# A hybrid attention block on one core: the written order around the MLA heads revised

## The chip, the core and the metric

The kernel runs on one core of one Trainium2 chip. The metric is the device time of one execution in microseconds; of several runs the median counts. Five engines work beside each other, each on its own queue, in order: TensorE (PE, with its weight loads PEld), VectorE (DVE), ScalarE (ACT), GpSimd (POOL) and SyncE (SP), which issues most of the transfers.

## The reference

One layer over 512 tokens of width 1024. The part that matters here is the attention block:

```python
h = rms_norm(x, attn_norm_g)
z = h @ w_in            # q-latent 256 | kv-latent 128 | rope key 32 | diff q 512 | diff k 512 | diff v 512
q = rms_norm(rms_norm(q_lat) @ w_uq);  k, v = (rms_norm(kv_lat) @ w_ukv) ...   # 8 MLA heads
probs = softmax(where(allowed, q k^T * scale, -1e30));  y_mla = probs @ v
q, k = rms_norm(dq), rms_norm(dk)                                              # 4 differential heads
logits = q k^T * scale + bias[t5_bucket(k_idx - q_idx)]                        # for m in (0, 1)
y_diff = rms_norm((probs[0] - lam * probs[1]) @ dv) * (1 - lam_init)
x = x + concat[y_mla, y_diff] @ w_out
```

A query sees the keys of its own and earlier chunks of 64. Behind it follow the convolutional feed-forward block and the gated embedding, which the change leaves alone. All products are kept to fp32 accuracy by splitting an operand into a rounded part and a remainder (`hi`, `lo`) and multiplying three times.

## The kernel before

Tokens lie in four tiles t of 128. The kernel begins with the latents (`zA`, banks for 416 columns of z), the up-projections of the MLA heads (`ukv`, `uq`) and the norms of their q and k. Then come the MLA heads in four pairs hp = 0 to 3, each with four query tiles t, so 16 steps i = 4 hp + t. One step, in the order in which the loop writes it:

- `mla_norm` scales the probabilities `pm` of tile t by the reciprocal of their sums (DVE). With t = 0 or 1 both heads of a pair lie in one bank and one reciprocal does for both; with t = 2 or 3 there are two of one column each.
- `mla_logits` multiplies the logits `ml` of tile t + 1 (PE), takes the row maxima (DVE), and `mla_exp` takes the exponentials (ACT), with their sums.
- At t = 2 and t = 3 PE transposes q and k of the next pair's two heads (`qT`, `kT`, or for the last pair `d0T`, `d1T` of the first diff head); ACT writes the rounded half into the tile `st`, DVE the remainder.
- Then stands what the table `extra` names for the step, a number of units of filling work for PE (`FILL_MLA`, by `pump`), and what `late` names.
- `mla_T` transposes the probabilities into one of the two banks `tp` (`pTm`), and a copy takes them to `pt`: on DVE for the pair's first head or t = 0, on ACT otherwise. `pt` has two buffers, and so has `tp`, which `qT`, `kT`, `d0T`, `d1T` and `pTm` share. `mla_pv` multiplies the probabilities of the step before with v, into the bank `mo`.

The filling work is z's diff columns (`zd_units`): q is `zd0*`, k `zd1*`, v `zd2*`, one tile for each t. A unit is six matmuls into one bank. When a tile is complete `zd_out` copies it out of the bank on ACT (`zd`), and for q and k squares it (ACT, `sq`) and sums the squares by head (DVE, `ssd`). Sums, a root on POOL (`zd_root`, a power, written to `rd`) and a scaling on DVE (`zd_scale`) make the norm. The weights come in tiles of 512 KB (`raw_d`, three buffers shared with `raw_o`), of which ACT makes the rounded half (`hi_d`) and DVE the remainder (`lo_d`), five buffers of each; W_out's are `raw_o`, `hi_o`, `lo_o` (o00 to o03 for the MLA half, o10 to o13 for the diff half).

`bias_strip` makes the diff heads' bias from a small table: 27 small POOL instructions into `vb` (a buffer of the pool of `sq`, which has two), three transfers on POOL's queue (to DRAM, spread over DRAM, back as `strip`), and a memset. `zd_root`'s power stands behind it on POOL.

Then come the 16 diff tiles (h, t), the logits two tiles ahead (`diff_logits`): DVE adds the bias and takes minima, ACT the exponentials, DVE combines the two maps (`pmd`, by `cf`). Between them the units are those of W_out (`wo_units`, banks `o`), for which `yh` and `yl` hold the two halves of the heads' outputs: 0 to 3 for MLA (`ym`, or the bank `mo3` for the last pair), 4 to 7 for diff.

What sets the order: PE's is the written one everywhere. In the region from the start to the line `region.__exit__` those of DVE, ACT and POOL are the written ones too; behind it a scheduler places them, and it may also put later instructions, such as the casts of W_out, between those of the region.

Of the kernel before, what the change touches and what calls it, by code (L numbers as in the profile page):

```python
# [12 lines left out]
F32R = mybir.dt.float32r  # L13
# [9 lines left out]
NT = 4  # L23
# [71 lines left out]
def hybrid_block(ctx: ExitStack, tc: tile.TileContext, a: dict, out: bass.AP):  # L95
# [294 lines left out]
    ssd, rd = small("ssd", [P, 2, NT, 8]), small("rd", [P, 2, NT, 8])  # L390
    def zd_out(c, t, ps):
        z_ = tt(f"zd{c}{t}")
        S.activation(z_, ps, AF.Identity, scale=rx[:, t:t + 1])
        zd[c].append(z_)
        if c < 2:
            sq = sq_tile("sq")[:, :T]
            S.activation(sq, z_, AF.Square)
            V.reduce_sum(ssd[:, c, t, :], sq.rearrange("p (m d) -> p m d", d=64), axis=AX.X)

    def zd_root(c):  # L400
        rms(up(rd[:, c]), up(ssd[:, c]), 8 * NT, 64)
# [196 lines left out]
    def mla_norm(hp, t):  # L598

        pm, pmf, sums, one = mla["pm", hp, t]  # L600
        ssum, rcp = sums[:, 1], sums[:, 2]
        for c in range(2):
            if not (c and one):
                w = slice(0, 2) if one else slice(c, c + 1)
                V.reciprocal(rcp[:, w], ssum[:, w])
            V.tensor_scalar(pm[c], pm[c], rcp[:, c:c + 1], None, op0=ALU.mult)

    def mla_T(hp, t):
# [100 lines left out]
    def diff_logits(h, t):  # L709
# [6 lines left out]
        for m in range(2):  # L716
            r = slice(64 * m, 64 * m + 64)
            ps = bank("lg", f"dl{h}{t}{m}")
            mm3(ps[:, :n], [(qh_[r, tsl[t]], ql_[r, tsl[t]], kh_[r, :n], kl_[r, :n])])
            pm = pm_tile("pmd")  # L720
            nm = sm.tile([P, 1], F32, tag="nm", bufs=4, name="nmd")
            V.tensor_tensor_reduce(out=pm[:, :n], in0=ps[:, :n], in1=strips[0][:, h, T - n:], scale=1.0, scalar=3e38, op0=ALU.add, op1=ALU.min, accum_out=nm)
            S.activation(pm[:, :n], pm[:, :n], AF.Exp, bias=nm, scale=-1.0, accum_out=s0 if m == 0 else s1)
            pms.append(pm)

        cf = sm.tile([P, 1], F32, tag="cf", bufs=4, name="cf")
        V.reciprocal(cf, s1)
        V.scalar_tensor_tensor(cf, cf, nlam, s0, op0=ALU.mult, op1=ALU.mult)
        V.scalar_tensor_tensor(pms[0][:, :n], pms[1][:, :n], cf, pms[0][:, :n], op0=ALU.mult, op1=ALU.add)
        df["pm", h, t] = pms[0]  # L730

    def diff_pv(h, t):
# [44 lines left out]
    def z2_hi(kq):  # L777
# [29 lines left out]
    mla_q(1)  # L807
    pump()
    mla_k(1)
    pump()  # L810
    mla_logits(0, 0)
    for c in range(2):
        mla_exp(0, 0, c)
    for hp in range(HP):
        for t in range(NT):
            i = NT * hp + t
            last = hp == HP - 1
            n = FILL_MLA[t]
            if t:
                mla_norm(hp, t)  # L820
            if t < NT - 1:
# [31 lines left out]
    pump(100)  # L853
    fill.append(wo_units(0, range(4), 4))
    diff_logits(0, 1)
    diff_T(1, 1)
    mla_pv(HP - 1, NT - 1)
    pump()
    y_hl(3, mla["po"])
    for i, (h, t) in enumerate(dslots):  # L860
        if i + 2 < len(dslots):
            diff_logits(*dslots[i + 2])
        pump(FILL_DIFF[h][t])
        df["pt", h, t] = probs_T(df.pop(("pm", h, t)), (t + 1) * P, f"d{h}{t}", True)
        if i:
# [672 lines left out]
```

## Time and profile before

| | us |
|---|---|
| runs, median of 3 (lowest, highest) | 648.82 (647.75, 649.01) |
| the profiled execution | 647.4 |
| its span, first to last instruction | 645.4 |
| PE busy | 633.0 |
| DVE busy | 486.7 |
| ACT busy | 360.6 |

The profile is one execution. The first two numbers of a row of instructions are its start and its duration, both in us from the span's start; an arrow in brackets says for how long the engine had been idle before it and what ended that. Matmuls overlap each other, so the distance between two starts, not the duration, says what a matmul takes of PE's time. The 16 MLA steps lie between about 71 and 161 us, the diff tiles between about 161 and 225 us.

### The profile page before, as it was taken

To read this page: it belongs to the slowest core of one execution; us is meant where nothing else is said; L and a number is where in the kernel's file an instruction comes from. 1 tells how busy PE (TensorE), PEld (TensorE's weight loads), DVE (VectorE), ACT (ScalarE), POOL (GpSimd) and SP (SyncE) were. 2 spreads that over 40 slices of the span, in tenths; PEclk is the share of its full clock that TensorE was granted. 3 is DMA by queue.
4 is the path that set the end of the run, shared out by engine and by line. 5 is a ranking of instruction groups with operands and counts; after the bars stand their busy time and mean duration, and the time that the engine had idled before them with its cause. 6 is when DMAs were issued, how large, how long until landed. Compare 5 with 4: busy or idle time off the path is not lost.

```text
span 645.4 us, 10213 instructions
## 1 busy us (share of the span) xinstructions
PE 633.0 (98%) x3900; PEld 555.6 (86%) x3900; DVE 486.7 (75%) x878; ACT 360.6 (56%) x629; POOL 67.3 (10%) x94
## 2 busy tenths in 40 slices
PE   9999998999999999999999999999999999999997
PEld 8988776887778887889999999999999999988886
DVE  6889666968878768888876767676767676769844
ACT  7897556548676364647554545555464545537211
POOL 1510044300000121001000000000011000000000
PEclk9999999999999999999999999999999999999999
DMA  8251222332410437636775646564646463531121
GB/s 299 104 164 39 92 76 104 99 131 73 125 34 2 163 107 236 164 72 175 190 202 130 180 118 186 127 191 115 180 115 180 115 180 115 180 130 53 39 89 50
DMA packets 29912, 82.63 MB, mean 128 GB/s; under 512 B 3100, under 2 KB 4124, under 8 KB 29736
## 3 DMA queue, kind: packets, MB, share of 16 engines
q1 hardware_dynamic: 23816, 69.17, 32.1%
q0 software_dynamic: 5616, 12.33, 11.3%
q8 instruction: 31, 0.51, 0.3%
q10 hardware_dynamic: 432, 0.49, 0.2%
q14 instruction: 17, 0.14, 0.1%
HBM read 77.77 MB, written 5.52 MB: 129 GB/s over the span
## 4 chain that ended last, share of the span: by engine, by line
PE 78%; DVE 9%; ACT 5%; DMA 4%; POOL 2%; issue 2%; ACTq 0%; DVEq 0%; POOLq 0%
PE dn L158 6%; PE dn L157 6%; PE dn L159 6%; PE gx L159 4%; PE gx L158 4%; PE gx L157 4%; PE g L157 3%; PE g L158 3%; PE g L159 3%; PE o L157 3%; PE o L159 2%; PE o L158 2%; PE pg L157 2%; PE pg L158 2%; PE pg L159 2%
## 5 line engine op out<-in xcount | busy, mean ns | idle before, releaser
L923 DVE TENSOR_TENSOR wSl<-rS,wSh 128x1024 fp32r<-128x1024 f32 x21 | 25.7, 1224 | 43.5 <-ACT wSh L919 43.3
L157 PE MATMUL dn<-ah,hi_dn 128*128 128x512 f32 x144 | 56.2, 391 | 0.0
L158 PE MATMUL dn<-al,hi_dn 128*128 128x512 f32 x144 | 56.2, 391 | 0.0
L159 PE MATMUL dn<-ah,lo_dn 128*128 128x512 f32 x144 | 56.0, 389 | 0.0
L1040 POOL DMA_DIRECT2D rS<-in_w_gu x19 | 22.7, 1194 | 250.4 <-DVE cv L1208 130.0
L919 ACT CAST wSh<-rS 128x1024 fp32r<-128x1024 f32 x21 | 22.0, 1047 | 35.8 <-PE gy L158 35.5
L157 PE MATMUL zd<-hi_d,xh 128*128 128x512 f32 x96 | 39.3, 410 | 0.0
L158 PE MATMUL zd<-lo_d,xh 128*128 128x512 f32 x96 | 37.7, 392 | 0.2 <-DVE lo_d L305 0.2
L674 DVE TENSOR_TENSOR x<-x,dn 128x512 f32<-128x512 f32 x44 | 29.9, 679 | 6.1 <-PE dn L159 6.1
L923 DVE TENSOR_TENSOR wTl<-rA,wTh 128x1024 fp32r<-128x1024 f32 x19 | 23.3, 1225 | 14.0 <-ACT wTh L919 13.5
L159 PEld LDWEIGHTS dn<-ah,lo_dn 128*128 128x128 f32 x144 | 27.0, 188 | 5.7
L157 PEld LDWEIGHTS dn<-ah,hi_dn 128*128 128x128 f32 x144 | 27.1, 188 | 5.2
L158 PEld LDWEIGHTS dn<-al,hi_dn 128*128 128x128 f32 x144 | 27.1, 188 | 4.9
L923 DVE TENSOR_TENSOR wAl<-rA,wAh 128x1024 fp32r<-128x1024 f32 x21 | 25.6, 1217 | 2.6 <-ACT wAh L919 2.6
L919 ACT CAST wAh<-rA 128x1024 fp32r<-128x1024 f32 x21 | 22.1, 1051 | 9.7 <-DMA rA<-in_w_gu 9.2
L1211 ACT ACTIVATE cv<-cv 128x512 f32<-128x512 f32 x22 | 13.9, 630 | 23.9 <-DVE cv L1208 23.8
L596 ACT ACTIVATE pm<-ml,sums,rq 128x128 f32<-128x128 f32 (+3 forms) x32 | 19.6, 617 | 13.4 <-DVE sums L579 8.6
L157 PE MATMUL g<-b2h,wAh 128*128 128x256 f32 (+1 forms) x88 | 26.4, 300 | 0.5 <-ACT g L1164 0.5
L157 PE MATMUL o<-yh,hi_o 128*128 128x512 f32 x64 | 26.9, 420 | 0.0
L159 PE MATMUL g<-b2h,wAl 128*128 128x256 f32 (+1 forms) x88 | 26.2, 297 | 0.0
L158 PE MATMUL g<-b2l,wAh 128*128 128x256 f32 (+1 forms) x88 | 26.2, 297 | 0.0
L1431 ACT ACTIVATE sg<-sg 128x512 f32<-128x512 f32 (+1 forms) x9 | 5.3, 584 | 36.8 <-DVE sg L1430 36.8
(475 smaller groups left out, 2215.7 us busy)
## 6 DMA issues: line engine op xcount, KB each, us to landing
rA<-in_w_gu SPq DMA_DIRECT2D x22, 512.0 KB, 4.0
rS<-in_w_gu SPq DMA_DIRECT2D x22, 512.0 KB, 3.7
rS<-in_w_gu POOLq DMA_DIRECT2D x19, 512.0 KB, 6.0
raw_dn<-in_w_down SPq DMA_DIRECT2D x18, 512.0 KB, 6.0
raw_d<-in_w_d SPq DMA_DIRECT2D x12, 512.0 KB, 4.1
r<-in_w_gu SPq DMA_DIRECT2D x19, 256.0 KB, 6.0
raw_o<-in_w_out SPq DMA_DIRECT2D x8, 512.0 KB, 3.7
rS_pg<-in_w_pg SPq DMA_DIRECT2D x6, 512.0 KB, 4.1
```

The costliest lines, as they stand in the source:

```text
L157: TE.matmul(ps, xh, wh, start=first and i == 0, stop=False, skip_group_check=again)
L158: TE.matmul(ps, xh, wl, start=False, stop=False, skip_group_check=again)
L159: TE.matmul(ps, xl, wh, start=False, stop=last and i == n - 1, skip_group_check=again)
L596: S.activation(pm[c], ps[c], AF.Exp, bias=nm[:, c:c + 1], scale=r[:, c:c + 1], accum_out=sums[:, 1, c:c + 1])
L674: V.tensor_tensor(xb(b), xb(b), ps, op=ALU.add)
L919: S.copy(h_, src)
L923: V.tensor_tensor(l_, src, _f32(h_), op=ALU.subtract)
L1040: nc.gpsimd.dma_start(sums[f].rearrange("p (i c) -> p i c", i=2), a["w_gu"][f][:, :2048].rearrange("p (i c) -> p i c", i=2)[:, :, :512], a ...
L1211: S.activation(cv, cv, AF.Silu)
L1431: S.activation(sg, sg, AF.Sigmoid)
```

## The change

Filling units: the number per step is now a table by pair and tile, two in every step of the first three pairs and one in every step of the last. Before it was 2, 1, 2, 2 in each pair. The number of units is the same; three go from the last pair to the three before.

Copies of z: those of k and v stand behind the copy of the transposed probabilities of the same step. The squares and sums of q and k move to steps 3 to 10, their scalings to steps 8 to 13 (before: squares with the copy, scalings in steps 6 to 12). The cast of z's last k weights goes ahead of the first exponentials.

GpSimd: the strip is made in step 0 (before: step 3).

Reciprocals: one for both heads in every step, behind the second head's sums.

First diff tiles: the written order of DVE, ACT and POOL reaches past the first two diff tiles, whose combination becomes a function of its own, and past the splits of the MLA outputs, which are written one by one. W_out's first weights are cast in steps 8 and 9; the remainder of a further one stands on DVE behind a tile's combination.

```diff
-FILL_MLA = (2, 1, 2, 2)
+FILL_MLA = ((2, 2, 2, 2), (2, 2, 2, 2), (2, 2, 2, 2), (1, 1, 1, 1))
     def zd_out(c, t, ps):
         z_ = tt(f"zd{c}{t}")
-        S.activation(z_, ps, AF.Identity, scale=rx[:, t:t + 1])
         zd[c].append(z_)
-        if c < 2:
-            sq = sq_tile("sq")[:, :T]
-            S.activation(sq, z_, AF.Square)
-            V.reduce_sum(ssd[:, c, t, :], sq.rearrange("p (m d) -> p m d", d=64), axis=AX.X)
+        zouts.append(lambda: S.activation(z_, ps, AF.Identity, scale=rx[:, t:t + 1]))
+        if c == 0:
+            z_flush()
...
+    def zd_sq(c, t):
+        sq = sq_tile("sq")[:, :T]
+        S.activation(sq, zd[c][t], AF.Square)
+        V.reduce_sum(ssd[:, c, t, :], sq.rearrange("p (m d) -> p m d", d=64), axis=AX.X)
...
         for c in range(2):
-            if not (c and one):
-                w = slice(0, 2) if one else slice(c, c + 1)
-                V.reciprocal(rcp[:, w], ssum[:, w])
+            if c == 0:
+                V.reciprocal(rcp, ssum)
             V.tensor_scalar(pm[c], pm[c], rcp[:, c:c + 1], None, op0=ALU.mult)
...
             w = wo_w(kq, dq)
+            if kq == 0 and dq + 1 in dqs:
+                with tc.issue_after(df["comb"].ins):
+                    wo_first[0, dq + 1] = wo_w(0, dq + 1)
...
     extra = {
-        0: [lambda: lo(*z1_hi(3))],
-        3: [bias_strip],
-        4: [lambda: zd_root(0), lambda: z2_hi(0)],
-        5: [lambda: z2_lo(0)],
-        6: [lambda: zd_scale(0, 0), lambda: z2_hi(1)],
-        7: [lambda: zd_scale(0, 1), lambda: z2_lo(1), lambda: z2_hi(2)],
-        8: [lambda: z2_lo(2), lambda: z2_hi(3), lambda: zd_root(1), lambda: zd_scale(0, 2), lambda: zd_scale(0, 3)],
-        9: [lambda: z2_lo(3)],
-        10: [lambda: zd_scale(1, 0)],
-        11: [lambda: zd_scale(1, 1)],
-        12: [load_x, lambda: zd_scale(1, 2), lambda: zd_scale(1, 3)],
+        0: [lambda: lo(*z13), bias_strip],
+        3: [sq(0, 0), zh(0)],
+        4: [zl(0), sq(0, 1), sq(0, 2), zh(1)],
+        5: [zl(1), sq(0, 3), lambda: zd_root(0)],
+        6: [sq(1, 0), zh(2)],
+        7: [zl(2), zh(3)],
+        8: [zl(3), sq(1, 1), zs(0, 0), first_hi],
+        9: [zl(4), sq(1, 2)],
+        10: [sq(1, 3), lambda: zd_root(1), zs(0, 1)],
+        11: [zs(0, 2), zs(0, 3)],
+        12: [load_x, zs(1, 0), zs(1, 1)],
+        13: [zs(1, 2), zs(1, 3)],
     }
     late = {
-        13: [lambda: y_hl(0, ymn[0])],
-        14: [lambda: y_hl(1, ymn[1]), lambda: y_hl(2, ymn[2]), first_o],
+        14: [yy(0)],
+        15: [yy(1)],
     }
...
     mla_k(1)
+    z13 = z1_hi(3)
...
                 if last:
-                    region.__exit__(None, None, None)
                     diff_logits(0, 0)
...
             mla_T(hp, t)
+            z_flush()
...
     diff_logits(0, 1)
+    mla_pv(HP - 1, NT - 1)
+    y_hl(3, mla["po"])
+    diff_comb(0, 0)
     diff_T(1, 1)
-    mla_pv(HP - 1, NT - 1)
+    y_hl(2, ymn[2])
+    diff_comb(0, 1)
+    region.__exit__(None, None, None)
     pump()
-    y_hl(3, mla["po"])
```

Three places show how the rows move; a number behind a name counts the buffers, and the first digits of a name give head pair and tile (`pTm120`: pair 1, tile 2, head 0).

DVE in the second pair at t = 2, behind the transposed q and k of head 4, before:

```order
L189 SCALAR_TENSOR_TENSOR st_123<-qT4_1252,qcol_117,st_123 96x512
L186 TENSOR_TENSOR st_123<-kT4_1260,st_123 96x512
L405 TENSOR_TENSOR zd00_789<-zd00_789,rd_394 128x512
L398 TENSOR_REDUCE ssd_393<-sq_1282 128x8
L398 TENSOR_REDUCE ssd_393<-sq_1293 128x8
L543 COPY pt_1300<-pTm120_1296 128x384
```

The same place after:

```order
L189 SCALAR_TENSOR_TENSOR st_123<-qT4_1265,qcol_117,st_123 96x512
L186 TENSOR_TENSOR st_123<-kT4_1273,st_123 96x512
L407 TENSOR_REDUCE ssd_393<-sq_1281 128x8
L552 COPY pt_1307<-pTm120_1303 128x384
L613 RECIPROCAL sums_1250<-sums_1250 128x2
```

The scaling of `zd00`, which reads POOL's `rd`, and one of two sums have left the place ahead of the copy of the transposed probabilities.

PE in the last pair at t = 0, ahead of the transposes of the probabilities, before (the tail of one unit, a whole one, and `pTm30`):

```order
L159 MATMUL zd23_1569<-hi_d20_1166,xh1l_139 128x512
L157 MATMUL zd22_1568<-hi_d21_1271,xh2_150 128x512
L158 MATMUL zd22_1568<-lo_d21_1272,xh2_150 128x512
L159 MATMUL zd22_1568<-hi_d21_1271,xh2l_151 128x512
L157 MATMUL zd22_1568<-hi_d21_1271,xh3_154 128x512
L158 MATMUL zd22_1568<-lo_d21_1272,xh3_154 128x512
L159 MATMUL zd22_1568<-hi_d21_1271,xh3l_155 128x512
L538 MATMUL pTm30_1647<-ident_112,pm_1606 128x128 x2
```

The same place after, with the tail of the logits:

```order
L159 MATMUL ml310_1626<-st_123 128x256
L157 MATMUL zd22_1531<-hi_d22_1286,xh4_167 128x512
L158 MATMUL zd22_1531<-lo_d22_1287,xh4_167 128x512
L159 MATMUL zd22_1531<-hi_d22_1286,xh4l_168 128x512
L157 MATMUL zd22_1531<-hi_d22_1286,xh5_171 128x512
L158 MATMUL zd22_1531<-lo_d22_1287,xh5_171 128x512
L159 MATMUL zd22_1531<-hi_d22_1286,xh5l_172 128x512
L547 MATMUL pTm30_1657<-ident_112,pm_1622 128x128 x2
```

One unit instead of two stands between the logits and the transposes.

ACT in the last pair at t = 1 and 2, before:

```order
L596 ACTIVATE pm_1678,sums_1665<-ml320_1666,sums_1665,rq_505 128x384
L596 ACTIVATE pm_1679,sums_1665<-ml321_1672,sums_1665,rq_505 128x384
L185 CAST yh0_1688<-ym0_1194 128x512
L541 COPY pt_1697<-pTm31_1692 128x512
L188 ACTIVATE st_123<-d0T0_1721,dcol_119 128x512
L596 ACTIVATE pm_1719,sums_1706<-ml330_1707,sums_1706,rq_505 128x512
```

The same place after:

```order
L605 ACTIVATE pm_1688,sums_1675<-ml320_1676,sums_1675,rq_505 128x384
L150 CAST hi_o03_2170<-raw_o03_2168 128x1024
L605 ACTIVATE pm_1689,sums_1675<-ml321_1682,sums_1675,rq_505 128x384
L550 COPY pt_1705<-pTm31_1700 128x512
L188 ACTIVATE st_123<-d0T0_1728,dcol_119 128x512
L605 ACTIVATE pm_1726,sums_1713<-ml330_1714,sums_1713,rq_505 128x512
```

The cast of W_out's fourth tile has come between the two heads' exponentials (before, it stood ahead of the copy of `pTm331`), and the split of the first pair's output has gone from there.

More of the change, by code (lines that the diff above doesn't have):

```diff
@@ L784, in hybrid_block, with first_hi @@
     z2_lo = lambda kq: lo(*z2_[kq])
-    extra = {
-        0: [lambda: lo(*z1_hi(3))],
-        3: [bias_strip],
-        4: [lambda: zd_root(0), lambda: z2_hi(0)],
-        5: [lambda: z2_lo(0)],
-        6: [lambda: zd_scale(0, 0), lambda: z2_hi(1)],
-        7: [lambda: zd_scale(0, 1), lambda: z2_lo(1), lambda: z2_hi(2)],
-        8: [lambda: z2_lo(2), lambda: z2_hi(3), lambda: zd_root(1), lambda: zd_scale(0, 2), lambda: zd_scale(0, 3)],
-        9: [lambda: z2_lo(3)],
-        10: [lambda: zd_scale(1, 0)],
-        11: [lambda: zd_scale(1, 1)],
-        12: [load_x, lambda: zd_scale(1, 2), lambda: zd_scale(1, 3)],
+    def first_hi():
+        raw = load_raw(a["w_out"][0, 0], 1024, "o00")
+        w = [wts.tile([P, 1024], F32R, tag=i, bufs=NW, name=f"{i}_o00") for i in ("hi", "lo")]
+        wo_first[0, 0] = w
+        z2_.append((*hi(raw, w[0]), w[1]))
+    sq, zs = (lambda c, t: lambda: zd_sq(c, t)), (lambda c, t: lambda: zd_scale(c, t))
+    zh, zl, yy = (lambda k: lambda: z2_hi(k)), (lambda k: lambda: z2_lo(k)), (lambda k: lambda: y_hl(k, ymn[k]))
+    extra = {
+        0: [lambda: lo(*z13), bias_strip],
[10 more added lines that the diff above has]
+        13: [zs(1, 2), zs(1, 3)],
     }
     late = {
-        13: [lambda: y_hl(0, ymn[0])],
-        14: [lambda: y_hl(1, ymn[1]), lambda: y_hl(2, ymn[2]), first_o],
+        14: [yy(0)],
+        15: [yy(1)],
     }
@@ L852, in hybrid_block @@
                     mla_exp(hp + 1, 0, c)
-    pump(100)
-    fill.append(wo_units(0, range(4), 4))
+    assert next(fill[0], None) is None
+    fill[:] = [wo_units(0, range(4), 4)]
     diff_logits(0, 1)
+    mla_pv(HP - 1, NT - 1)
+    y_hl(3, mla["po"])
+    diff_comb(0, 0)
     diff_T(1, 1)
-    mla_pv(HP - 1, NT - 1)
+    y_hl(2, ymn[2])
+    diff_comb(0, 1)
+    region.__exit__(None, None, None)
     pump()
-    y_hl(3, mla["po"])
     for i, (h, t) in enumerate(dslots):
@@ L862, in hybrid_block @@
             diff_logits(*dslots[i + 2])
+            diff_comb(*dslots[i + 2])
         pump(FILL_DIFF[h][t])
```

11 lines of the change are left out of this document (9 added, 2 removed).

## The prediction

> **What bounds the kernel now.** I read the page's first part, then the busy time by stretches, then PE's waits in the stretch that the change touches.
>
> ```profile
> span 645.4 us, 10213 instructions
> ...
> PE 633.0 (98%) x3900; PEld 555.6 (86%) x3900; DVE 486.7 (75%) x878; ACT 360.6 (56%) x629; POOL 67.3 (10%) x94
> ...
> 63.00:92.60 29.60, 27.91 (x166) 21.78 (x163) 20.15 (x45) 15.88 (x34) 8.03 (x29) 1.00 0.19 57
> 92.60:116.40 23.80, 21.69 (x145) 17.12 (x143) 16.53 (x40) 14.84 (x31) 6.54 (x3) 1.00 0.37 119
> 116.40:137.70 21.30, 21.30 (x145) 17.23 (x143) 16.86 (x41) 11.90 (x27) 6.41 (x1) 1.00 0.36 125
> 137.70:163.00 25.30, 24.15 (x171) 19.42 (x172) 20.81 (x54) 18.39 (x43) 0.00 (x0) 1.00 0.33 105
> 163.00:240.00 77.00, 76.85 (x446) 62.00 (x445) 62.35 (x159) 46.56 (x107) 8.25 (x7) 1.00 0.25 79
> ```
>
> The columns behind a stretch are its length and the busy us of PE, PEld, DVE, ACT and POOL, then PE's clock, the DMA share and GB/s. PE is busy for 633.0 of 645.4 us, and the change takes no matmul away. So all it can win is PE's idle time where it moves something: 1.7, 2.1, 0.0 and 1.2 us in the four MLA stretches, 0.15 in the diff tiles. That is 5.1 at most, 0.8% of the span. PE's waits from 63 to 163 us name nearly all of it (waited for, total us, times, longest):
>
> ```profile
> PE kT L557 <- DVE pt L543: 1.5, 1, 1.5
> PE d1T L704 <- ACT pt L541: 1.2, 1, 1.2
> PE kT L557 <- ACT pt L541: 0.6, 1, 0.6
> PE qT L550 <- ACT pt L541: 0.6, 1, 0.6
> PE qT L550 <- DVE st L189: 0.5, 1, 0.5
> PE pTm L538 <- DVE st L189: 0.3, 1, 0.3
> PE zd L158 <- DVE lo_d L305: 0.2, 1, 0.2
> ```
>
> They sum to 4.9 us. Six of the seven are transposes that wait for a bank of `tp`, whose last reader stands in DVE's or ACT's queue behind work that nobody needs yet.
>
> **The change, part by part.** *The strip earlier on POOL: 1.5 us.* The largest wait ends this chain:
>
> ```profile
> 55.74 0.95 DVE L524 TENSOR_REDUCE ssq<-sqq 128x8 f32<-128x768 f32 x1
> ...
> 81.90 6.63 POOL L641 TENSOR_SCALAR vb<-tab 4x207 f32<-4x207 f32 x27 [46.45 <-DVE sums L605]
> ...
> 95.90 0.17 DVE L164 TENSOR_SCALAR rs_m<-ssd 128x32 f32<-128x32 f32 x1
> ...
> 104.62 5.47 POOL L165 TENSOR_TENSOR rd<-rs_m,mhalf 128x32 f32<-128x32 f32 x1
> ...
> 110.12 0.69 DVE L405 TENSOR_TENSOR zd<-zd,rd 128x512 f32<-128x512 f32 x1 [3.70 <-POOL rd L165]
> ```
>
> The root's input is ready at 96.1, but POOL takes it up at 104.6, since the strip is ahead of it; DVE then stands for 3.7 us before `zd00`, with the copy of `pTm120` behind it, and PE with it. After the change POOL's queue has the same rows in the same order (27 instructions, three DMAs, the memset, two roots), but `vb` waits for less: its buffer's reader is now a sum over `sqq` that ends at 56.7, where before it was the sum of `zd10`. From 81.9 to 104.6 the strip took 22.7 us; begun at 56.7 it ends near 79.4, and begun only in step 0, near 73.5, at 96.2. Either way it is over when the root wants POOL, now a step later, and `zd00`'s scaling stands two steps further on. A root of 5.5 fits. Gain 1.5; at worst, if POOL were still late, 0. The three DMAs go with it, into a stretch where the DMA share was 0.19.
>
> *Squares, sums and copies of z moved: 2.2 us.* The other five waits of the first two pairs are each one queue.
>
> ```profile
> 65.64 0.69 DVE L398 TENSOR_REDUCE ssd<-sq 128x8 f32<-128x512 f32 x1 [0.56 <-ACT sq L397]
> ...
> 80.46 0.63 ACT L397 ACTIVATE sq<-zd 128x512 f32<-128x512 f32 x1
> 81.00 0.57 ACT L541 COPY pt<-pTm 128x512 f32<-128x512 f32 x1
> ...
> 109.31 0.63 ACT L397 ACTIVATE sq<-zd 128x512 f32<-128x512 f32 x1
> ```
>
> The 0.5 of `qT`: DVE's remainder for the first `st` stood behind the last of four sums, which waited 0.56 for ACT; all four go. The 0.6 of `kT`: ACT's copy of `pTm01` stood behind a copy of z and this square; the copy now goes first. The 0.6 of `qT`, the same: ACT's copy of `pTm121` stood behind a cast, two copies of z and two squares, of which a cast and one square are left. The 0.2 of `lo_d`: the cast of z's last k weights is now ahead of the exponentials. The 0.3 of the transposed probabilities is met by one more unit on PE just ahead, 1.4 us (below). Together 2.2, with 1.5 that makes 3.7. What the moved work costs where it lands: in the worst step, the fifth, DVE has a sum more than before, 0.69, and PE a unit more. Copies of a `pt` at t = 3 wait for the product that frees the buffer anyway. So I take 0; the ends are 0 and 0.7, one sum in front of one copy.
>
> *The last pair, three units fewer: 1.4 us of new waits, 1.2 us taken away.*
>
> ```profile
> 139.10 0.40 PE L157 MATMUL zd<-hi_d,xh 128*128 128x512 f32 x1
> ...
> 140.49 0.39 PE L157 MATMUL zd<-hi_d,xh 128*128 128x512 f32 x1
> ...
> 141.85 0.38 PE L538 MATMUL pTm<-ident,pm 128*128 128x128 f32 x2
> ...
> 140.48 0.48 DVE L606 TENSOR_SCALAR pm<-pm,sums 128x128 f32<-128x128 f32 x2
> ```
>
> A unit takes 140.49 - 139.10 = 1.39 us of PE. At t = 0 two stood between the logits and `pTm30`; with one, PE is there at 140.49, while DVE scales the two halves from 140.48 to 140.96. First new wait: 0.4 (0.2 for the first half to 0.5 for both).
>
> ```profile
> 145.80 0.67 ACT L596 ACTIVATE pm<-ml,sums,rq 128x384 f32<-128x384 f32 x1
> ...
> 147.71 0.15 DVE L605 RECIPROCAL sums<-sums 128x1 f32<-128x1 f32 x1
> ...
> 150.35 0.74 DVE L189 SCALAR_TENSOR_TENSOR st<-d0T,dcol,st 128x512 fp32r<-128x512 f32 x1
> 151.06 0.69 DVE L186 TENSOR_TENSOR st<-d1T,st 128x512 fp32r<-128x512 f32 x1
> ...
> 151.76 0.81 PE L538 MATMUL pTm<-ident,pm 128*128 128x128 f32 x6
> ...
> 158.63 1.05 ACT L150 CAST hi_o<-raw_o 128x1024 fp32r<-128x1024 f32 x1 [0.67 <-DMA raw_o<-in_w_out]
> 159.59 0.58 ACT L541 COPY pt<-pTm 128x512 f32<-128x512 f32 x1
> ```
>
> At t = 2 `pTm320` and `pTm321` need the banks of `d0T0` and `d1T0`, free when DVE's remainders end at 151.1 and 151.75; with two units between, PE came at 151.76, just in time. With one it comes 1.39 earlier. DVE comes hardly earlier: the split `yh0l` has left, but the scalings of `zd12` and `zd13` (two at 0.69) stand there, and the second exponential, which ended near 146.5, now comes behind the cast of o03: 1.05, and that cast waits until PE has read z's third v weights, at the end of the unit behind the logits. Its sums are thus ready near 147.6, and since both reciprocals are one now, the scaling starts where it did. What DVE wins is one reciprocal, 0.2. PE is also 0.4 late from the first wait, but DVE's maxima follow PE, so that does not close the gap. PE at 150.37 against 150.9: 0.5, then the second bank, which frees 0.7 after the first while three transposes take 0.4 (half of 0.81): 0.3. Second new wait: 0.8 (0 if the cast is not late, 1.4 if a whole unit's cover is gone). At t = 3 the copy of `pTm330` stands behind a split that waits for ACT, but PE has 12 products and the logits of a diff tile to do: 0.2 (0 to 0.7, one split). Against these 1.4 the wait of 1.2 goes: there ACT stood at 158.63 for the transfer of o03, issued only at 155.05 when a buffer came free, with the copy of `pTm331` behind. The cast now stands further up, and its buffer frees with `lo_o00`, four steps before.
>
> *The diff tiles: 0.* There PE idled 0.15 in 77 us. DVE loses eight reciprocals in MLA and gets the same work here in another order. The remainders o01 to o03, and so the buffers for o10 to o13, come later, so ACT's casts may again wait for a transfer:
>
> ```profile
> raw_o<-in_w_out SPq DMA_DIRECT2D x8, 512.0 KB, 3.7
> ```
>
> Such a wait cost PE 1.2 once, where the copy behind it was wanted at once. Here logits run two tiles ahead. I take 0, with 1.2 as the far end. The loads of x move behind one more weight load on SP's queue; x is first wanted when `o00` is summed, so 0.
>
> Sum: 1.5 + 2.2 + 1.2 - 1.4 = 3.5 us. The span goes from 645.4 to 641.9, the profiled execution from 647.4 to 643.9. The median of the runs, 648.8, lies 1.4 above the profiled one, so I put the median at 645.3.
>
> **A rule against it.** `vb` moves into a stretch where DVE is full. What the rows show of the two engines beside each other:
>
> ```profile
> 119.61 1.22 DVE L305 TENSOR_TENSOR lo_d<-raw_d,hi_d 128x1024 fp32r<-128x1024 f32 x1
> ...
> 124.42 1.23 DVE L305 TENSOR_TENSOR lo_d<-raw_d,hi_d 128x1024 fp32r<-128x1024 f32 x1
> ...
> 121.00 6.41 POOL L165 TENSOR_TENSOR rd<-rs_m,mhalf 128x32 f32<-128x32 f32 x1 [10.91 <-DVE rs_m L164]
> ...
> 56.60:63.20 6.60, 6.25 (x21) 1.00 0.00 0
> ```
>
> The second `lo_d` runs inside POOL's root, the first ahead of it: 1.23 and 1.22. The root took 6.41 here and 5.47 where DVE stood idle. So it is POOL that pays. The Trainium skill, "SBUF — State Buffer", section "Who interferes with whom", says that a DVE instruction with two SBUF inputs contends with a GpSimd instruction that reads SBUF, and whoever comes first blocks the other for its whole length. By it the sum would hold only if the small instructions slip between DVE's; the rows agree in part, since only POOL shows a loss.
>
> **The rivals.** *The last pair starves* (same sign, smaller). For it: DVE is busy for 20.8 of 25.3 us there, and the pair loses 3 x 1.39 = 4.2 us of cover. Against it: three remainders of W_out leave that stretch. If the new waits double to 2.8, the gain is 2.1: 646.7.
>
> *No new waits.* If DVE is ahead, as in the third pair, where PE never waited: gain 4.9, 643.9.
>
> *DVE is blocked by `vb`.* In 56.6 to 63.2 DVE has 21 instructions; if each waits for one of the 27 on POOL (6.63 / 27 = 0.25), 5.2 us. The four sums that left (4 x 0.69) cover 2.8, so 2.4 come to PE: gain 1.1, 647.7. This is what the Trainium skill's rule ("SBUF — State Buffer") would make of it at worst.
>
> *The change doesn't do it.* If POOL's root still comes late, for want of the buffer or by a slow transfer, 1.5 stay, and the gain is 2.0: 646.8.
>
> *Slower: ACT waits for W_out.* o10 to o13 and two more loads each start when a remainder ends, and ACT's cast stands in a fixed place. If each costs what o03's did, 6 x 1.2 = 7.2 against 3.5: 652.5. It decides from the third such wait (no gain left), and the kernel is measurably slower from the fifth. Against it: the far-ahead logits, and ACT busy for only 46.6 of 77 us.
>
> **How the numbers follow.** My forecast has 0.52, no new waits 0.13, starving 0.15, DVE blocked 0.05, change not done 0.06, slower 0.09. About 0.2%, 1.3 us, is what a measurement tells here. Faster: 0.52 + 0.13 + 0.12 of starving + 0.03 + 0.05 of the next two = 0.85. Slower: 0.06 of the last. The rest, 0.09, is the same. The range: all new waits at 0 gives 643.9, less 0.4 for the scatter of the runs, 643.5; the new waits at their far ends (0.5 + 1.4 + 0.7) and one ACT wait of 1.2 leave 4.9 - 2.6 - 1.2 = 1.1, 647.7. That leaves out the slower case and little else.
>
> **What the changed profile would show.** Right: no DVE row that waits for POOL's `rd`; `vb` near 57 and the strip's memset near 80; PE without idle time from 63 to the end of the third pair, and the third pair ending 3.7 us earlier less the three units moved ahead; in the last pair waits of PE at `pTm` of t = 0 for DVE's scaling and at t = 2 for DVE's `st`, about 1.4 us; no wait at `d1T`. Wrong: a wait of 2 us or more in the last pair, DVE rows near 57 to 63 longer than before, or ACT rows in the diff tiles that end on a transfer, with PE's `do` or `pTd` behind them.

## The result, and the profile after

The changed kernel takes 644.6 us (median of 4 runs, 643.78 to 644.82), the kernel before, run beside it, 648.9 (647.75 to 649.06). The ratio is 0.9935, with a 95% interval of 0.9918 to 0.9952. Run again beside later kernels, it took 644.07 against 648.78, ratio 0.993 (0.9911 to 0.995). So it is faster, by 4.3 and 4.7 us; 645.3 was predicted. The granted clock of a run is its mean TensorE clock as a share of full speed. Of all runs of the kernel before, here and below, 49 list it, and they fall into two groups, both found on each of the four chips listed: 25 at 0.998 or 0.999 with a median of 647.12 us, 24 at 0.994 to 0.997 with 648.97, while the ten runs of the kernel after all have 0.998 to 1.000 and a median of 644.37. The profiled execution took 644.8, and its page begins:

```profile
span 643.0 us, 10203 instructions
...
PE 632.4 (98%) x3900; PEld 556.2 (87%) x3900; DVE 486.9 (76%) x870; ACT 360.2 (56%) x629; POOL 69.2 (11%) x94
```

The span fell by 2.4 us and PE's busy time hardly. The stretches, with the boundaries and columns of the prediction:

```profile
63.00:92.60 29.60, 29.60 (x183) 24.59 (x182) 18.27 (x40) 15.59 (x33) 3.79 (x10) 1.00 0.44 135
92.60:116.40 23.80, 23.80 (x156) 19.47 (x155) 19.02 (x43) 16.84 (x38) 5.47 (x1) 1.00 0.22 67
116.40:137.70 21.30, 21.30 (x144) 17.43 (x143) 17.59 (x38) 14.31 (x29) 5.80 (x1) 1.00 0.39 123
137.70:163.00 25.30, 23.82 (x167) 17.99 (x168) 20.16 (x56) 16.41 (x42) 0.00 (x0) 1.00 0.06 23
163.00:240.00 77.00, 75.39 (x435) 60.87 (x432) 61.70 (x154) 47.42 (x107) 9.10 (x8) 1.00 0.30 100
```

PE no longer idles in the first three stretches (1.7 and 2.1 us before). In the last pair it idles for 1.5, and in the diff tiles, where it idled for 0.15, for 1.6. PE's waits from 63 to 240 us (waited for, total us, times, longest) say on what:

```profile
PE dl L159 <- DVE st L189: 0.9, 2, 0.6
PE mo L633 <- DVE pt L552: 0.7, 1, 0.7
PE pTd L547 <- ACT pt L550: 0.5, 1, 0.5
PE pTm L547 <- DVE st L189: 0.4, 1, 0.4
PE pTm L547 <- DVE pm L614: 0.3, 1, 0.3
```

None of the seven old waits is there. Three of the five lines are the last pair's (`mo`, `pTm`, 1.4 us), two are new waits of the diff tiles (1.4 us). Both sets stand in the second profile of the same kernel, with 1.1 in place of 0.9.

Where the time went is best read from the starts of three matmuls that every version has: the first four transposes `qT`, ahead of the MLA steps, the first product of `o00` behind them, and `pp` behind the diff tiles. Before, and then after:

```profile
62.74 0.60 PE L550 MATMUL qT<-ident,qn 128*96 128x128 f32 x4
...
161.83 0.50 PE L157 MATMUL o<-yh,hi_o 128*128 128x512 f32 x1
...
236.26 0.39 PE L157 MATMUL pp<-pk 128*128 128x512 f32 x1
```

```profile
62.58 0.60 PE L559 MATMUL qT<-ident,qn 128*96 128x128 f32 x4
...
156.89 0.47 PE L157 MATMUL o<-yh,hi_o 128*128 128x512 f32 x1
...
233.84 0.39 PE L157 MATMUL pp<-pk 128*128 128x512 f32 x1
```

The stretch from `qT` to `o00`, called MLA from here on, went from 99.09 to 94.31 us, 4.78 less. The stretch from `o00` to `pp`, called the diff tiles, went from 74.43 to 76.95, 2.52 more. So the net is 2.26 us, nearly the whole difference of the spans.

### The profile page after: what moved, and what is told of

Read it like the earlier page. It is cut to its first block, busy times and chain, and to the rows that moved or that the text cites. A ratio compares the mean times of both kernels' runs of the same rounds, so it can differ in the third digit from the quotient of the medians.

```text
span 643.0 us, 10203 instructions
## 1 busy us (share of the span) xinstructions
PE 632.4 (98%) x3900; PEld 556.2 (87%) x3900; DVE 486.9 (76%) x870; ACT 360.2 (56%) x629; POOL 69.2 (11%) x94
## 4 chain that ended last, share of the span: by engine, by line
PE 86%; DVE 7%; ACT 3%; issue 2%; DMA 1%; ACTq 0%; DVEq 0%; SPq 0%
PE dn L157 6%; PE dn L158 6%; PE dn L159 6%; PE gx L159 4%; PE gx L158 4%; PE gx L157 4%; PE zd L157 3%; PE zd L159 3%; PE zd L158 3%; PE g L157 3%; PE g L158 3%; PE g L159 3%; PE pg L159 2%; PE pg L158 2%; PE pg L157 2%; PE o L157 2%
## 5 line engine op out<-in xcount | busy, mean ns | idle before, releaser
L734 ACT ACTIVATE pmd<-pmd,nmd 128x128 f32<-128x128 f32 (+3 forms) x32 | 17.9, 560 | 15.1 <-DVE nmd L733 15.0
```

## The experiments

Theory: the gain is the MLA waits, each with its own queue as its cause, less what the last pair and the diff tiles give back. Rivals: one part alone carries it (the strip, or the copies), the fixed order of the first diff tiles is part of the gain, or the three units moved are.

All twelve runs, with the two distances of each profiled execution, in us. The kernel before was run beside each group of kernels, so its median is given too. Its 53 runs lie between 646.6 and 650.5, so the distances are the finer measure. The ratio is estimated from the runs, with its interval; it is not exactly the quotient of the two medians.

| kernel | median (before beside it) | ratio (95% interval) | qT to o00 | o00 to pp |
|---|---|---|---|---|
| before | | | 99.09 | 74.43 |
| after | 644.60 (648.91) | 0.9935 (0.9918 to 0.9952) | 94.31 | 76.95 |
| e_strip | 645.81 (648.17) | 0.9969 (0.9958 to 0.9979) | 97.35 | 74.49 |
| e_z | 644.40 (648.17) | 0.995 (0.9935 to 0.9965) | 96.23 | 74.48 |
| e_diffold | 643.86 (648.17) | 0.9943 (0.9926 to 0.9961) | 95.48 | 74.60 |
| e_fill | 645.42 (648.17) | 0.9958 (0.994 to 0.9976) | 95.14 | 77.40 |
| e_striplate | 644.45 (647.81) | 0.9946 (0.9929 to 0.9963) | 94.26 | 76.88 |
| e_early | 643.65 (647.81) | 0.9934 (0.9916 to 0.9953) | 94.24 | 75.91 |
| e_fillflush | 644.21 (647.81) | 0.9939 (0.9921 to 0.9958) | 93.34 | 76.40 |
| e_b3 | 644.29 (647.81) | 0.9942 (0.9925 to 0.996) | 93.33 | 77.17 |
| after_again | 644.07 (648.78) | 0.993 (0.9911 to 0.995) | 94.24 | 77.05 |
| e_b4 | 643.22 (648.78) | 0.9913 (0.9894 to 0.9932) | 94.46 | 74.59 |
| e_b5 | 642.75 (648.78) | 0.991 (0.9889 to 0.9931) | 94.45 | 74.50 |
| e_b6 | 641.95 (648.44) | 0.9901 (0.9882 to 0.992) | 93.63 | 74.48 |

### e_strip: the strip alone

```diff
-        0: [lambda: lo(*z1_hi(3))],
-        3: [bias_strip],
+        0: [lambda: lo(*z1_hi(3)), bias_strip],
```

> The kernel before with one edit: the strip's instructions move from step 3 to step 0. Theory (the gain is the sum of MLA waits, each with a cause of its own): POOL is through with the strip when the root's input comes, the root runs at about 96 to 102, DVE no longer stands 3.7 us for rd, and the 1.5 us of kT go: 1.5 us faster than before, 647.4. Rival (the queues around the squares are the cause, the strip is not): the wait at kT stays or moves to the next transpose, under 0.4 us faster.

The distance fell by 1.74 us, the span by 1.5, the ratio says 2.0 (1.4 to 2.7). POOL's rows:

```profile
64.97 8.15 POOL L641 TENSOR_SCALAR vb<-tab 4x207 f32<-4x207 f32 x27 [29.38 <-DVE ssd L398]
...
95.89 5.46 POOL L165 TENSOR_TENSOR rd<-rs_m,mhalf 128x32 f32<-128x32 f32 x1 [6.01 <-DVE rs_m L164]
```

The root runs 8.7 us earlier than the 104.62 of before, as soon as its input is there, and the wait of `kT` for DVE's `pt` falls from 1.5 to 0.2. Five of the other six waits stay. The sixth, 0.5 of the second `qT` for DVE's `st`, has fallen below what is listed, but not by the edit: DVE is 0.2 us sooner there, and was so already ahead of the strip's first instruction. Between the first and the second `qT` lie 3.95 us here and 4.29 before; without these 0.34 the distance falls by 1.40. So 1.3 to 1.4 of the 1.5 is shown for the strip.

### e_z: the copies, squares, sums and scalings of z alone

The functions `zd_out`, `z_flush` and `zd_sq` and the steps 0 to 13 of `extra` are the kernel after's; the strip stays in step 3, and `first_o`, the table of units, the reciprocals and the diff tiles are the kernel before's.

> The kernel before with the z part alone: copies of k and v behind the copy of the transposed probabilities, squares, sums and scalings in the later steps, the cast of z's last k weights ahead; the strip stays in step 3, units, reciprocals and diff tiles as before. Theory as the prediction had it: 2.2 us from the squares and copies, and since zd00's scaling now stands two steps further on, the late root is covered as well: up to 3.7 us faster than before, 645.2. Rival (the strip is needed): the wait for rd only moves to step 8 and 1.5 us stay: 2.2 us faster, 646.7.

The distance fell by 2.86 us. PE's waits in the MLA steps:

```profile
PE zd L157 <- ACT zd L394: 2.5, 2, 1.3
PE d1T L713 <- ACT pt L550: 1.1, 1, 1.1
```

All six waits that the prediction gave to the strip and to the copies are gone, the 1.5 us of `kT` too, although the strip stands in step 3. A new one of 2.5 has come, so the time lies between theory (3.7) and rival (2.2). With the diff tiles as before, e_z is 2.8 us ahead of the kernel before by the distances, and 0.55 ahead of the whole change. So the first rival holds: one part alone carries the net gain. The table of units, the reciprocals, `first_hi` and the first diff tiles together win another 1.92 us in MLA and give 2.47 back in the diff tiles. That the strip's own edit is not needed here, and that the late copies have a price, is taken up by the next two runs.

### e_striplate: the kernel after with the strip in step 3

```diff
-        0: [lambda: lo(*z13), bias_strip],
-        3: [sq(0, 0), zh(0)],
+        0: [lambda: lo(*z13)],
+        3: [sq(0, 0), zh(0), bias_strip],
```

> The kernel after with the strip's instructions back in step 3. Theory: zd00's scaling now stands in step 8, so even a late root is covered, and the strip's early place adds nothing: the time of the kernel after, within 0.4 us (4.3 us faster than before). Rival (the prediction's sum, in which the strip has 1.5 us of its own): 1.5 us slower than after, 2.8 faster than before.

The time of the kernel after: 94.26 us and 76.88. But the reason is another than the one expected:

```profile
59.95 8.85 POOL L649 TENSOR_SCALAR vb<-tab 4x207 f32<-4x207 f32 x27 [24.03 <-DVE ssq L533]
...
102.15 5.47 POOL L165 TENSOR_TENSOR rd<-rs_m,mhalf 128x32 f32<-128x32 f32 x1 [15.85 <-DVE sums L613]
```

The strip runs early all the same. POOL has nothing ahead of it, so the step in which it is written sets little (59.95 in place of 56.34). What held it until 81.9 us before was its buffer, in the pool of the squares: the sum that read the square ended at 81.8. Now all squares but one are written behind the strip, that one takes the other buffer, and the strip waits only for a sum `ssq`, made ahead of the MLA steps. So moving the strip's line and moving the squares are two ways to the same 1.5 us, and together they bring it once. Whether `zd00`'s later scaling would hide a late root was not tried, since the root is never late here.

### e_fill: the kernel after with the old units

```diff
-FILL_MLA = ((2, 2, 2, 2), (2, 2, 2, 2), (2, 2, 2, 2), (1, 1, 1, 1))
+FILL_MLA = ((2, 1, 2, 2),) * 4
```

> The kernel after with the old table of units, 2, 1, 2, 2 in each pair. Theory: the last pair's three new waits (1.4 us) go, the 0.3 us of the transposed probabilities in the first pair comes back, the diff tiles keep theirs: 1.1 us faster than after, 643.5. Rival (the three units in the first pairs are what filled their waits): 1 to 2 us of waits return in the first two pairs, 645 to 646.

The time is the rival's (645.42), and the waits came back where it says, but not the old ones. The last pair's waits fell from 1.4 to 0.2 us, as the theory says, yet MLA became 0.83 us longer, by one wait of 1.22 in each of the first two pairs. PE and ACT around the first:

```profile
81.15 0.40 PE L159 MATMUL zd<-hi_d,xh7l 128*128 128x512 f32 x1
...
82.75 0.81 PE L547 MATMUL pTm<-ident,pm 128*128 128x128 f32 x6
83.49 0.66 PE L633 MATMUL mo<-pt,kvb 128*64 128x128 f32 x8
85.38 0.50 PE L157 MATMUL zd<-hi_d,xh 128*128 128x512 f32 x1 [1.22 <-ACT zd L394]
```

```profile
84.25 0.48 ACT L550 COPY pt<-pTm 128x384 f32<-128x384 f32 x1 [1.76 <-PE mo L633]
84.63 0.69 ACT L394 ACTIVATE zd<-zd,rx 128x512 f32<-128x512 f32 x1
```

The tile of z ends at about 81.5, but its copy stands behind that of the transposed probabilities, which waits for the product that frees `pt`. The next pair of z's tiles wants the bank with the first unit of the next step. With two units in each step, a pair of tiles ends together, and a step's logits and products lie ahead of the next pair. So it is the even table that keeps the late copies from costing anything here: it saves two waits of 1.22 and costs the last pair 1.2.

### e_fillflush: the old units, and two copies ahead

```diff
-FILL_MLA = ((2, 2, 2, 2), (2, 2, 2, 2), (2, 2, 2, 2), (1, 1, 1, 1))
+FILL_MLA = ((2, 1, 2, 2),) * 4
...
+            if i in (2, 6):
+                z_flush()
             mla_T(hp, t)
             z_flush()
```

> The kernel after with the old table of units (2, 1, 2, 2) and z's copies ahead of the copy of the transposed probabilities in the two steps whose bank the next unit wants (2 and 6). Theory: with the old table alone PE waited twice 1.2 us for a bank of z that ACT's copy had not emptied; with the copy ahead both go, and the last pair keeps its second units, so its 1.4 us stay away too: 2.4 us faster than with the old table alone, 1.5 faster than after, 5.8 faster than before. Rival (a copy of z ahead brings back the old waits at kT and qT): at least 1 us of that is lost, no faster than after.

MLA takes 93.34 us, 1.80 less than with the old table alone and 0.97 less than after. The first of the two waits is gone; of the second, 0.8 us stay, and the prize is smaller by that. The runs show little of it: 644.21 against the 644.45 of e_striplate, which has the distances of the kernel after and ran on the same chip.

### e_diffold: the first diff tiles as before

`region.__exit__` stands ahead of the first diff logits again, the combination is inside `diff_logits`, the splits are at their old places, and the lines with `issue_after` in `wo_units` are out.

> The kernel after with the first diff tiles as in the kernel before: the region ends ahead of the first diff logits, combinations inside the logits' function, the splits at their old places, and W_out's remainders not tied to a tile's combination (o00's cast and remainder stay in steps 8 and 9). Theory: the diff tiles give back 2.5 us in the kernel after, because W_out's remainders, and with them the buffers for o12 and o13, come late; here they come in the MLA steps, so PE's waits at dl and pTd between 175 and 206 us go: 1.3 to 2.5 us faster than after, 642.1 to 643.3. Rival (the fixed order is a part of the gain): new waits in the last pair of 1 to 2 us take the place, 645.5 or more.

The diff tiles take 74.60 us, as before the change, and not one wait of PE is listed from 163 to 240. But MLA is 1.17 longer: the last pair's waits grew from 1.4 to 2.2 us. So theory and rival each had a part; by the distances 1.2 us were won, and the median (643.86) lies between the two forecasts.

```profile
PE pTm L547 <- DVE st L189: 1.3, 1, 1.3
PE pTm L547 <- DVE pm L614: 0.7, 1, 0.7
PE d1T L712 <- ACT pt L550: 0.2, 1, 0.2
```

What has moved between the two stages shows in DVE's busy time from `o00` to `pp`, third number behind the comma, before, after and here:

```profile
161.83:236.26 74.43, 74.28 (x435) 59.88 (x433) 60.39 (x157) 45.41 (x109) 7.97 (x7) 1.00 0.27 86
```

```profile
156.89:233.84 76.95, 75.34 (x436) 60.24 (x434) 64.48 (x163) 45.61 (x107) 7.96 (x7) 1.00 0.28 93
```

```profile
158.61:233.21 74.60, 74.45 (x435) 60.01 (x433) 59.32 (x155) 44.32 (x108) 7.97 (x7) 1.00 0.22 73
```

DVE has 4.1 us more in the diff tiles after than before, and 5.2 more than here. A remainder of W_out is 1.22 us. Four of the eight stood ahead of `o00` before, only one does in the kernel after, and five here: three of them are 3.7 of the 4.1. The edit takes both away from the diff tiles, this work and the late buffers, so it doesn't tell the two apart.

### e_early: W_out's remainders earlier in the diff tiles

```diff
             diff_comb(*dslots[i + 2])
+            if i < 3:
+                with tc.issue_after(df["comb"].ins):
+                    wo_first[0, i + 1] = wo_w(0, i + 1)
```

(and the three lines in `wo_units` out)

> The kernel after with one edit: W_out's remainders o01, o02, o03 stand behind the combinations of the diff tiles (0,2), (0,3), (1,0), where in the kernel after they come as the units reach them, up to five tiles later. Theory: the buffers for o11 to o13 come free earlier, ACT's casts no longer wait 0.7 and 1.4 us for a transfer, and PE's three waits between 179 and 203 us go, 2.5 us by the distances of the starts: 2.5 us faster than after, 6.8 faster than before. Rival (DVE has no room: it is busy for four fifths of that time, the remainders only push another row): waits of 1 us or more at other dl or pTd, gain under 1 us.

The diff tiles take 75.91 us, 1.04 less, of 2.5 expected. In the kernel after, two casts of ACT waited for a transfer, ahead of PE's two later waits (0.33 at 197.42 and 0.47 at 203.16):

```profile
189.19 1.05 ACT L150 CAST hi_o<-raw_o 128x1024 fp32r<-128x1024 f32 x1 [0.67 <-DMA raw_o<-in_w_out]
...
192.93 1.05 ACT L150 CAST hi_o<-raw_o 128x1024 fp32r<-128x1024 f32 x1 [1.45 <-DMA raw_o<-in_w_out]
```

They are the prediction's slower rival in small. The profile's chain of work that ended last runs through the second transfer (4.29 us from 188.61) and its cast to PE's wait at 203.16. With the remainders earlier no cast of W_out waits there (one waits 0.41 at 169.04), and PE's two later waits are gone too. The third, at `dl`, stays:

```profile
PE dl L159 <- DVE st L189: 0.5, 1, 0.5
PE dl L157 <- DVE nmd L730: 0.2, 1, 0.2
```

The second row is new. All seven remainders still lie behind `o00`, and DVE is busy for 63.8 us there. So about 1.0 of the 2.5 went with the later place of the remainders, and 1.5 stayed; theory and rival each had a part. That the 1.0 is the transfers' and the 1.5 the work's is likely, but not shown. The runs show 0.8 of it: 643.65 against the 644.45 of e_striplate on the same chip.

### e_b3: the three together

The edits of e_fillflush and e_early, and `yy(1)` moved ahead of `diff_logits(0, 0)`.

> The last two edits together, and the split of the second pair's output ahead of the first diff logits instead of behind them. If each is worth what it is alone: 1.5 + 2.5 = 4.0 us faster than after, 8.3 faster than before, and PE idle for under 0.5 us between 63 and 240. Rival (DVE and ACT have no room for all of it): half of that.

MLA 93.33, diff tiles 77.17: the 0.97 us of the one came, the 1.04 of the other did not. The first wait of `dl`, 0.71 at 166.08, is new, and the second has grown to 1.31:

```profile
PE dl L159 <- DVE st L189: 2.0, 2, 1.3
```

By the distances that is 0.8 us ahead of the kernel after, where 4.0 was expected and 2.0 by the rival; the medians (644.29, and 644.45 for e_striplate) show 0.2. The rival's reason fits the rows: the first remainder behind `o00` starts at 164.15 here and at 164.19 in e_early, though `o00` starts 1.08 sooner, and the first `dl` waits for the `st` right behind it. PE is there sooner and DVE is not. That speaks for the work of the remainders as what costs there, though their place, and the moved `yy(1)`, are not excluded; the next runs put four of them back ahead of `o00`.

### after_again, e_b4 and e_b5: the remainders back in a last pair with its second units

e_b4 joins the edits of e_diffold and e_fillflush. e_b5 moves, besides, squares and scalings of q and k one step ahead (the lines against e_b4):

```diff
-        7: [zl(2), zh(3)],
-        8: [zl(3), sq(1, 1), zs(0, 0), first_hi],
-        9: [zl(4), sq(1, 2)],
-        10: [sq(1, 3), lambda: zd_root(1), zs(0, 1)],
-        11: [zs(0, 2), zs(0, 3)],
-        12: [load_x, zs(1, 0), zs(1, 1)],
-        13: [zs(1, 2), zs(1, 3)],
+        7: [zl(2), sq(1, 1), zh(3)],
+        8: [zl(3), sq(1, 2), zs(0, 0), first_hi],
+        9: [zl(4), sq(1, 3), lambda: zd_root(1)],
+        10: [zs(0, 1), zs(0, 2)],
+        11: [zs(0, 3), zs(1, 0)],
+        12: [load_x, zs(1, 1), zs(1, 2)],
+        13: [zs(1, 3)],
```

> The kernel after once more, unchanged, beside the kernels of this call: 644.6, a ratio of 0.9935 to before. Its second profile: if the three waits in the last pair (1.4 us) and the three in the diff tiles (1.4 us) belong to the written order and not to the one execution, they stand there again, each within 0.1 us; if they are chance, others stand in their place.

> The first diff tiles as before the change together with the old table of units and z's copies ahead in steps 2 and 6. Theory (the remainders o01 to o03 cost 1.9 us in the last pair where it has one unit a step, and 2.5 us in the diff tiles, but nothing in a last pair that has its second units): MLA as short as with the copies ahead (93.3 us from qT to o00, against 94.3 in the kernel after), the diff tiles as before (74.5 us from o00 to pp, against 76.9): 3.3 us faster than after, 7.6 faster than before. Rival (DVE has no room for the remainders wherever they stand): new waits of 2 us or more in the last pair, no more than 1.3 us faster than after.

> The same with the squares and scalings of z's q and k each one step earlier from step 7 on, which takes two scalings (1.3 us of DVE) out of the last pair. Theory: if DVE still holds up PE in the last pair, up to 0.5 us faster than without this; if not, the same within 0.4 us. Rival: the squares on ACT and DVE in the second pair bring back waits at kT or qT, 0.5 us or more slower.

The kernel after repeats its waits within 0.2 us (0.1 was expected) and its distances within 0.1. e_b4 has 94.46 and 74.59: MLA as in the kernel after, and the diff tiles as before the change, 2.2 us less in all (3.3 expected). The missing 1.1 is MLA's. The edit of e_diffold, which brings four remainders ahead of `o00`, made MLA 1.17 longer with one unit in the last pair's steps, and makes it 1.12 longer here, with second units (94.46 against the 93.34 of e_fillflush). So the theory's "nothing" did not come, and the second units do not cover the remainders; nor did the rival's waits of 2 us come. Little of the 1.12 is listed as waits: 0.4 at `d1T` has come and 0.2 at `mo` has gone, beside the 0.8 of e_fillflush in the second pair. The move pays because the diff tiles win more than the last pair loses, 1.81 us here and 2.35 in e_diffold. The runs show 0.85 us of the 2.2 for e_b4 and 1.3 for e_b5, whose six runs (642.42 to 643.46) all lie below the six of the kernel after (643.47 to 644.96). Between e_b4 and e_b5 the distances differ by 0.1: the scalings did not hold anything up.

### e_b6: the fastest

The lines against e_b5:

```diff
-        6: [sq(1, 0), zh(2)],
-        7: [zl(2), sq(1, 1), zh(3)],
-        8: [zl(3), sq(1, 2), zs(0, 0), first_hi],
-        9: [zl(4), sq(1, 3), lambda: zd_root(1)],
-        10: [zs(0, 1), zs(0, 2)],
+        6: [sq(1, 0)],
+        7: [sq(1, 1), zh(2)],
+        8: [zl(2), sq(1, 2), zs(0, 0), zh(3)],
+        9: [zl(3), sq(1, 3), lambda: zd_root(1), first_hi],
+        10: [zl(4), zs(0, 1), zs(0, 2)],
```

> The same once more, with the casts of z's v weights k2 and k3 and of o00 one step later. In the trace without this, ACT has a cast of 1.04 us ahead of the two copies of z in step 6, and PE waits 0.8 us for the second of them. Theory: that wait goes, 0.8 us less from qT to o00 (93.7 us against 94.45), 0.8 us faster. Rival: the remainders, one step later too, come late for the units, or DVE's later queue holds up the last pair: no gain.

The expected 0.8 came: 93.63 us and 74.48, and one wait of PE is left between 63 and 240:

```profile
PE d1T L712 <- ACT pt L550: 0.4, 1, 0.4
```

Its median is 641.95 us (641.05 to 642.35, 5 runs), 6.5 less than before beside it and 2.1 less than the kernel after, which ran on another chip. It beats both kernels.

## Why the prediction came out as it did

**The total.** 645.3 was forecast and 644.6 measured; the sign and the range hold, and so does the kind of mechanism, waits taken from MLA less some given back behind it. That the number came so near is luck: two errors cancel. The gain was forecast as 3.5 us, and the distances give 2.3, the spans 2.4, the profiled executions 2.6 (647.4 and 644.8). And the prediction took the 1.4 by which the median of before lies above its profiled execution for the kernel after as well, whose median lies 0.2 below its profiled one. The gap goes with the granted clock: the profiled execution of before (0.998) belongs to the group at 647.12, and about half of its runs are slower at a lower clock, while none of the ten runs of the kernel after has one. Within 0.998 to 1.000 the gain is 647.12 - 644.37 = 2.75, near what the traces tell. The rest of the 4.3 goes with the lower clock of the kernel before; why that kernel has it so often (24 of 49 runs, against 4 of the 82 runs of all others) is open.

**The seven waits.** All are gone, 4.9 us by the list. In the distances they weigh more, so PE's idle time, which the prediction took for the most that could be won (5.1), is no ceiling. The wait for `lo_d`, before and after:

```profile
76.11 0.39 PE L157 MATMUL zd<-hi_d,xh 128*128 128x512 f32 x1
76.73 0.50 PE L158 MATMUL zd<-lo_d,xh 128*128 128x512 f32 x1 [0.23 <-DVE lo_d L305]
```

```profile
75.32 0.39 PE L157 MATMUL zd<-hi_d,xh 128*128 128x512 f32 x1
75.55 0.40 PE L158 MATMUL zd<-lo_d,xh 128*128 128x512 f32 x1
```

The starts are 0.62 apart with the wait and 0.23 without: 0.39 lost, where the row names 0.23. The 0.16 between is the overlap of two matmuls, 0.39 less 0.23, which a wait takes away as well. If every wait costs this much more, which is an estimate from this one place, seven waits lost and three gained are 0.6 us more than the list's 3.5, of the 4.8 measured. The other 0.7 is not traced to rows.

**The strip, 1.5.** e_strip shows 1.3 to 1.4 of it, and the reason that the prediction named, a buffer whose reader ends earlier, is the one in the trace. But moving the squares frees the buffer as well (e_z, e_striplate), so the headings of 1.5 and 2.2 are not two separate edits.

**Squares and copies, 2.2, at a cost of 0.** The gain came. For the 0.3 of the transposed probabilities the prediction relied on one more unit of PE's, but e_z and e_fill, without that unit, do not have the wait either. The cost is 0 only with the even table: e_z and e_fill show 2.4 to 2.5 us of waits for a bank of z without it. The prediction looked at what the moved copies stand behind in ACT's queue, not at who wants the bank they empty.

**The last pair, 1.4.** It was 1.4, with 0.3, 0.4 and 0.7 where 0.4, 0.8 and 0.2 were forecast, so that the sum fits is chance. The last is off because DVE's `yh1l` waited 1.24 us for ACT's half, behind two exponentials of the first diff tile. The wait at `d1T` went as forecast.

**The diff tiles, 0.** This step failed: it was 2.5 us, beyond the far end of 1.2. It said that DVE "gets the same work here in another order"; it got three remainders more, and with them 4.1 us of work, on an engine with 14 us to spare in 74. The prediction did say that the remainders come later, but priced only the transfers that wait for their buffers, and DVE's own time at nothing. ACT's casts did wait for transfers, as the slower rival has it; with these two waits gone 1.0 of the 2.5 came back in e_early, and none in e_b3, where another cast waits 1.20 at 169.16. In e_diffold, where four of the remainders are elsewhere, 2.35 came back. So DVE's lateness is likely the larger part; no run parts the two.

**The other rivals.** The last pair did not starve (1.4 against 2.8). `vb` held DVE up far less than its rival says. The rows before, with POOL at rest, and after, with `vb` from 56.3:

```profile
56.94 0.69 DVE L501 TENSOR_TENSOR kvb<-kvb,rq 128x512 f32<-128x512 f32 x1
```

```profile
56.34 7.92 POOL L649 TENSOR_SCALAR vb<-tab 4x207 f32<-4x207 f32 x27 [21.02 <-DVE ssq L533]
```

```profile
56.51 0.84 DVE L510 TENSOR_TENSOR kvb<-kvb,rq 128x512 f32<-128x512 f32 x1
...
61.73 1.22 DVE L305 TENSOR_TENSOR lo_d<-raw_d,hi_d 128x1024 fp32r<-128x1024 f32 x1
```

`kvb` grew from 0.69 to 0.84, and two rows behind it (`rt`) from 0.42 to 0.51 and from 0.28 to 0.33; `lo_d` took 1.22 before too, and the small rows are as long as before. All ten runs in which `vb` starts near 56 or 57 have these lengths, and e_strip, e_z and e_striplate, where it starts later, have those of before. So DVE lost about 0.3 us where the rival has 5.2; this sign of being wrong, DVE rows near 57 to 63 that are longer, did show, small as it is, and no wait of PE from 50 to 63 is listed behind it. POOL lost more (the last section). The Trainium skill, "SBUF — State Buffer", section "Who interferes with whom", calls the port pair that DVE and GpSimd share an exclusive lock. The rows agree in that each side is held up; DVE's longest loss in a row is 0.15 us.

## What to carry to other kernels

When work is moved to close waits of the bounding engine, count each other engine's busy time in the stage that receives it: here a stage in which DVE was busy for four fifths of the time became 2.5 us longer with 4.1 us more of DVE's work, half of what was won ahead of it. A copy that empties a bank has two that depend on its place, the queue it stands in and the next owner of the bank; a table of filling work has to fit both. Start-to-start distances between marks that all versions share tell the stages apart when the runs scatter by more than the effect. And when two kernels are compared by medians, compare their granted clocks too: here some 1.5 of 4.3 us went with them.

## What the hardware showed that was not expected

POOL's time grew by about the whole length of each remainder that DVE made beside it, or somewhat more. The 27 instructions of `vb` took 6.63 us before, with no `lo_d` beside them; 7.92 and 8.15 in after and e_strip, with one; 8.85 and 9.02 in e_striplate and e_z, with two. In e_z the two are:

```profile
61.87 1.22 DVE L305 TENSOR_TENSOR lo_d<-raw_d,hi_d 128x1024 fp32r<-128x1024 f32 x1
...
66.66 1.21 DVE L305 TENSOR_TENSOR lo_d<-raw_d,hi_d 128x1024 fp32r<-128x1024 f32 x1
```

```profile
59.78 9.02 POOL L650 TENSOR_SCALAR vb<-tab 4x207 f32<-4x207 f32 x27 [24.10 <-DVE ssq L533]
```

9.02 less 6.63 is 2.4, twice the 1.2 of a remainder. DVE was not busier in e_z than before (6.35 of 9.02 us, 5.23 of 6.70), so it is the kind of its work that tells. Which kind is open: in the kernel after 6.63 and one remainder are 7.85 of the 7.92, so `kvb` and `rt`, which also have two tensors as inputs, cost POOL next to nothing, and it was DVE that lost there.

In the place where it was measured, a wait cost PE 0.16 us more than its row names (0.39 against 0.23), since the overlap of neighbouring matmuls is lost with it.
